# Routing queries in plain float32, and gate one-hots of four tokens in one comparison

## The chip, the cores and the metric

The kernel runs on one core of a Trainium2 chip. The metric is the device time in microseconds of one execution. Five engines work side by side, each through its own queue in order: TensorE (PE, with its weight loads as PEld), VectorE (DVE), ScalarE (ACT), GpSimd (POOL) and SyncE (SP), which issues most transfers.

## What is computed

One layer of a hybrid encoder over 1,024 tokens of width 1,024, then a final RMSNorm. A token mixer (stick-breaking attention and a gated delta net, merged by gates) and a cross-attention into 256 memory tokens come first. The third part, PEER retrieval, is the one that changes:

```
q = (xt @ w_pq).reshape(T, 8, 2, 128)              # routing queries
s = einsum('thpd,hpnd->thpn', q, subkeys)          # 128 scores per head and half
top_s, top_i = top_k(s, 16)
cand_s = top_s[:, :, 0, :, None] + top_s[:, :, 1, None, :]
best_s, best_pos = top_k(cand_s, 16)
expert = the pair of keys at best_pos;  gate = softmax(best_s)
act = gelu(einsum('thkd,td->thk', peer_u[expert], x)) * gate
out = einsum('thk,thkd->td', act, peer_v[expert])
```

## The kernel before

Tokens are worked in three groups, 256, 384 and 384 of them. Each group goes through token mixing, cross-attention and `routing`. A float32 product is made of three fast ones: `split` (lines 85 to 91) writes a value as a high and a low part, the high part by a copy on ScalarE (line 77), the low part by a subtraction on VectorE or GpSimd (line 89), and `mm3` (line 223) multiplies high by high, low by high and high by low. `proj` (from line 226) does this for each 128 columns of a weight matrix, which it loads as the tile `raw` and splits into `wh` and `wl`.

In `routing` the norm gives the activations `xn` and their parts `xhi` and `xlo` (in the last group `xh` and `xl`, which are kept). `proj` goes through the sixteen 128-column tiles of `w_pq`. For each tile ScalarE copies the queries out, TensorE multiplies them with the sub-keys (line 678), and `best` (lines 655 to 665) searches the sixteen best of 128 scores on VectorE, with five passes for each block of 128 tokens. The load of the next group's tokens (line 449, tile `gc`) waits for the last of these searches, because it takes over their memory.

Blocks 4, 5 and 6 of 128 tokens are retrieved by dense products over all 16,384 experts, the other five by gathers of expert rows (line 778), which GpSimd issues from the middle of the second group on, between everything else; VectorE reduces a gathered row in line 794 or adds it in line 83, TensorE weights it in line 823. For the dense blocks `spread` builds a matrix of gates: for each token a one-hot over the first key, times the gate (`o0`, line 898, VectorE), and a one-hot over the second key (`o1`, for even tokens on GpSimd in line 903, for odd ones in two steps on ScalarE), which TensorE multiplies (line 904). Four tokens share one PSUM bank, which ScalarE copies to `st`; with 384 tokens there are 96 such steps. Block 4's steps come from stored choices (`pick_stored`); those of blocks 5 and 6 follow their own choice (`pick_gates`) and are mixed with `dense_ahead`, which makes the first 36 of 128 dense tiles. `dense` then goes through all 128 tiles, mixed with the rest of the gathers.

The order of each engine's queue is written ahead of time by a planner that goes by its own costs for every instruction and keeps to the dependencies; nothing is reordered at run time.

Of the kernel before, what the change touches and what calls it, by code (L numbers as in the profile page):

```python
# [20 lines left out]
P = 128  # L21
# [15 lines left out]
OBS = 12  # L37
# [14 lines left out]
def block_kernel(ctx: ExitStack, tc: tile.TileContext, x_t, mem_t, gains, cst, sel, eye, w_in, conv, a_log,  # L52
# [22 lines left out]
    # ---- small helpers  # L75
# [42 lines left out]
    def mix(a, b, ratio):  # L118
        """Steps of a and b in turn, ratio of a for each of b."""
# [21 lines left out]
    # ---- constants  # L141
# [43 lines left out]
    # ---- scratch in DRAM  # L185
# [15 lines left out]
    # ---- building blocks  # L201
    def norm_t(hi, lo, tmp, xs, gi, n, keep=None):
        """RMSNorm over the partitions and tiles of xs(k), [P, n] each, split in two parts."""
# [7 lines left out]
        for k in range(KD):  # L211
            whole = keep is not None and keep.shape[2] == n
            y = keep[:, k] if whole else tmp.tile([P, n], F32, name="sq", bufs=2)
            stt(y, xs(k), gn[:, gi, k:k + 1], rs, OP.mult, OP.mult)
            split(hi[:, k], lo[:, k], y)
            if keep is not None and not whole:
                pool.tensor_copy(keep[:, k], y[:, n - keep.shape[2]:])
# [8 lines left out]
    def proj(w, col0, ncol, hi, lo, n, kt=KD, share=0):  # L226
        """Yields (tile index, product) for each 128 columns of w, transposed: [columns, tokens]. GpSimd splits
        every share-th tile of w."""
# [35 lines left out]
    # ---- stick-breaking attention of one 128-query block, four heads at a time, keys on partitions  # L264
    def stick(tmp, kT, vN, qT, sbo, e, qb, t0):
# [4 lines left out]
        for kb in range(qb, -1, -1):  # L270
# [6 lines left out]
            # softplus; for large z the logarithm is z itself  # L277
# [26 lines left out]
    # ---- gated delta net over one 128-token chunk, four heads together  # L304
    class Chunk:
# [67 lines left out]
        def inverse(self):  # L373
            """Inverse of (I + A) by doubling of diagonal blocks, and its transpose; AT holds -A transposed."""
# [26 lines left out]
            # keys and values with tokens on partitions  # L401
# [15 lines left out]
        def scan(self, S, S2, o):  # L417
            """Recurrence over chunks."""
# [17 lines left out]
    def token_mixing(g, t0, T, x1_where, result):  # L436
# [3 lines left out]
        with ExitStack() as eo:  # L440
# [11 lines left out]
            # gated delta net: projections, short convolution  # L452
# [9 lines left out]
            # beta and decay logits  # L462
# [65 lines left out]
            with ExitStack() as es:  # L528
                tmp = open_pool(f"d2{g}", 2, where=es)
                # output gate and branch gates wait in DRAM  # L530
# [104 lines left out]
    def routing(g, x1, t0, T, where, kept=None):  # L635
        """Returns the pool that choose() goes on with, and by block the best scores and keys."""
# [8 lines left out]
        if kept:  # L645
            hi, lo = kept
            n0 = sum(t0 // P + b in DENSE for b in range(NB)) * P
        else:
            n0 = 0
        with ExitStack() as es:  # L650
# [16 lines left out]
            xn = p1.tile([P, KD, T - n0], F32, name="xn")  # L667
            sk = p1.tile([P, 16, P], F32, name="sk")
            sp.dma_start(sk, subk)
            if not kept:  # L670
                hi, lo = p1.tile([P, KD, T], F32R, name="xhi"), p1.tile([P, KD, T], F32R, name="xlo")
            norm_t(hi, lo, tmp, lambda k: x1[:, k], 3, T, keep=xn)
            for i, ps in proj(w_pq, 0, 2048, hi, lo, T, share=SH_R):
# [8 lines left out]
            for src, dst in ((xn, xn_sc), (x1, xr_sc)):  # L682
                for b in range(NB):
# [4 lines left out]
                    c0 = b * P - (n0 if src is xn and kept else 0)  # L688
                    bs = slice(c0, c0 + P)
# [9 lines left out]
    def choose(tmp, tv, ti):  # L699
        """The sixteen best sums per head of one 128-token block. A pair (a, b) of ranks can be among them  # L700
        only with (a + 1) * (b + 1) <= 16: a < 4 with all b, or b < 4."""
# [21 lines left out]
        # gate: softmax over the chosen sixteen (the first is the largest)  # L723
# [7 lines left out]
        # position -> ranks -> expert  # L731
# [43 lines left out]
    # ---- retrieval by gathering expert rows  # L775
# [6 lines left out]
    def retrieve_u(blk, keep):  # L782
        """Expert activations of one block; tokens on partitions, one slot per gather."""
# [25 lines left out]
    def retrieve_v(blk, keep):  # L809
        """Weighted sum of expert rows, residual and final norm; slots on partitions, one token per gather."""  # L810
# [22 lines left out]
    def retrieve_y(blk, keep):  # L833
        """The same with tokens on partitions, one slot per gather."""
# [26 lines left out]
    def finish(y, ps, r0):  # L861
        """Final norm of 64 tokens, 32 w + p: quarter d of the channels of token (w, p) is y[32 d + p, w]."""
# [11 lines left out]
    # ---- retrieval by dense products over all experts, for the last tokens  # L874
    def choose_t(p2, tv, ti):
        """Keys and gates of one block with the slots on partitions."""
# [8 lines left out]
    def spread(px_, sel3, b):  # L885
        """Gates as a matrix: g_sc[c, i, r, t] is the gate of token 32 * c + t for expert 128 * r + i, zero if not
        chosen."""
        neg = px_.tile([P, 3, P], F32, name="neg")
        vec.tensor_scalar(neg[:, 0], sel3[:, 1], -1.0, None, op0=OP.mult)
        for c0 in range(0, P, 32):  # L890
            st = px_.tile([P, P, 32], F32, name="st")
            for c in range(c0, c0 + 32, 4):
                ps = by4(a_tile())
                for j in range(4):
                    o0 = px_.tile([P, P], F32, name="o0", bufs=OBS)
                    o1 = px_.tile([P, P], F32, name="o1", bufs=OBS)
                    t = c + j
# [225 lines left out]
```

## Time and profile before

| | us |
|---|---|
| median of three runs | 3813.43 (3813.3 to 3814.75) |
| span of the profiled execution, 56,994 instructions | 3821.6 |
| routing, first group (about) | 444 to 519 |
| routing, second group (about) | 1293 to 1413 |
| routing, third group (about) | 2324 to 2462 |
| spread (line 904), first to last | 2435 to 2808 |
| dense products (line 975), first to last | 2841 to 3779 |

The profiled execution was not timed beside its profile; its span stands 8.2 us over the median of the runs. Busy time is how long an engine had work running. Matmuls overlap each other, so the duration shown for one is longer than the distance from it to the next.

### The profile page before, as it was taken

Reading aid. Unit: us, or ns where it says so; the run is one execution under the profiler, and the core shown is the slowest. Engines: PE = TensorE matmul, PEld = TensorE weight load, DVE = VectorE, ACT = ScalarE, POOL = GpSimd, SP = SyncE. Lnnn points to the kernel's source line nnn. Section 1 sums busy time; section 2 is a strip of 40 time slices with the busy share of each in tenths; the row PEclk is TensorE's granted clock in tenths of the full one; section 3 lists DMA queues with packets and bytes.
Section 4 is the critical chain, followed back from the end, with each engine's and each line's share of the span. In section 5 each row is a group of like instructions: output and inputs, shape, how many; then the busy total and the mean of one; then the engine's idle time right before and its main releaser. Section 6 shows DMA issues by size and latency. Waiting matters only on the chain. (4 is left out here: it accounts for less than half of the span.)

```text
span 3821.6 us, 56994 instructions
## 1 busy us (share of the span) xinstructions
PE 3402.2 (89%) x20621; PEld 2852.3 (75%) x20621; DVE 2852.1 (75%) x5650; ACT 1624.2 (43%) x2992; POOL 1993.3 (52%) x1611
## 2 busy tenths in 40 slices
PE   7998977898889987999978899989769999999995
PEld 6888866787767765767766667878758888888884
DVE  6445699886566799427896667998767888887886
ACT  5754543664313333545523233556633333333333
POOL 1010007666754546467686455788964545544553
PEclk9999988998989988999979899999969999999997
DMA  6537539987899998989878989998999999999996
GB/s 163 147 92 210 151 110 316 332 293 235 290 353 300 347 335 282 307 301 305 263 248 288 345 301 341 305 315 275 325 316 330 340 339 347 339 327 321 360 386 236
DMA packets 745796, 1100.56 MB, mean 288 GB/s; under 512 B 42149, under 2 KB 554533, under 8 KB 742441
## 3 DMA queue, kind: packets, MB, share of 16 engines
q0 software_dynamic: 184320, 671.17, 49.4%
q1 hardware_dynamic: 561192, 425.73, 36.4%
q8 instruction: 163, 2.67, 0.3%
q14 instruction: 121, 0.98, 0.1%
HBM read 1036.60 MB, written 60.16 MB: 287 GB/s over the span
## 5 line engine op out<-in xcount | busy, mean ns | idle before, releaser
L778 POOL DMA_INDIRECT row<-in_peer_u_dram,ix x640 | 818.7, 1279 | 525.5 <-DVE y L83 146.9
L794 DVE CUSTOM_DVE_ANT_0 row<-row,xs 128x1024 f32<-128x1024 f32 x640 | 818.8, 1288 | 123.5 <-DMA row<-in_peer_u_dram,ix 100.9
L223 PE MATMUL pj<-xhi,wh 128*128 128x384 f32 (+1 forms) x1912 | 636.3, 333 | 52.9 <-ACT xhi L77 20.6
L223 PE MATMUL pj<-xhi,wl 128*128 128x384 f32 (+1 forms) x1912 | 637.0, 333 | 26.6 <-POOL wl L89 16.6
L89 DVE TENSOR_TENSOR wl<-raw,wh 128x1024 fp32r<-128x1024 f32 (+1 forms) x420 | 489.9, 1167 | 227.5 <-ACT wh L77 203.7
L778 POOL DMA_INDIRECT row<-in_peer_v_dram,it x384 | 448.6, 1168 | 358.3 <-PE ac L823 169.0
L223 PE MATMUL pj<-xlo,wh 128*128 128x384 f32 (+1 forms) x1912 | 621.4, 327 | 6.4 <-DVE xlo L89 6.4
L77 ACT ACTIVATE wh<-raw 128x1024 fp32r<-128x1024 f32 (+1 forms) x447 | 449.8, 1007 | 276.2 <-PE pj L223 176.5
L778 POOL DMA_INDIRECT row<-in_peer_v_dram,ix x256 | 352.0, 1375 | 346.7 <-DVE y L83 171.9
L223 PE MATMUL pj<-xh,wh 128*128 128x384 f32 x1152 | 399.9, 347 | 44.6 <-ACT h L80 41.6
L223 PEld LDWEIGHTS pj<-xhi,wh 128*128 128x128 f32 x1912 | 371.1, 194 | 89.6 <-ACT xhi L77 26.8
L223 PEld LDWEIGHTS pj<-xhi,wl 128*128 128x128 f32 x1912 | 370.9, 194 | 65.2 <-POOL wl L89 19.5
L223 PE MATMUL pj<-xh,wl 128*128 128x384 f32 x1152 | 398.8, 346 | 4.3 <-POOL wl L89 3.4
L223 PE MATMUL pj<-xl,wh 128*128 128x384 f32 x1152 | 393.1, 342 | 0.0
L223 PEld LDWEIGHTS pj<-xlo,wh 128*128 128x128 f32 x1912 | 369.4, 194 | 23.2 <-issue 10.6
L83 DVE SCALAR_TENSOR_TENSOR y<-row,hh,y 128x1024 f32<-128x1024 f32 x256 | 329.1, 1285 | 14.6 <-DMA row<-in_peer_v_dram,ix 13.1
L823 PE MATMUL ac<-row,sb 128*32 128x256 f32 x3072 | 267.0, 408 | 51.1 <-DMA row<-in_peer_v_dram,it 45.9
L89 POOL TENSOR_TENSOR wl<-raw,wh 128x1024 fp32r<-128x1024 f32 x27 | 66.0, 2443 | 428.1 <-DVE one L758 330.5
L77 ACT ACTIVATE vh<-vr 128x1024 fp32r<-128x1024 f32 x128 | 134.8, 1058 | 322.9 <-PE pj L975 311.6
L223 PEld LDWEIGHTS pj<-xh,wh 128*128 128x128 f32 x1152 | 220.3, 191 | 66.3 <-ACT h L80 56.9
L223 PEld LDWEIGHTS pj<-xh,wl 128*128 128x128 f32 x1152 | 220.7, 192 | 20.0 <-POOL wl L89 4.2
L89 DVE TENSOR_TENSOR vl<-vr,vh 128x1024 fp32r<-128x1024 f32 x128 | 156.5, 1223 | 90.7 <-ACT vh L77 79.3
(453 smaller groups left out, 6583.7 us busy)
## 6 DMA issues: line engine op xcount, KB each, us to landing
raw<-in_w_in_dram SPq DMA_DIRECT2D x132, 512.0 KB
raw<-in_peer_ut_dram SPq DMA_DIRECT2D x128, 512.0 KB
vr<-in_peer_v_dram SPq DMA_DIRECT2D x128, 512.0 KB
raw<-in_w_pq_dram SPq DMA_DIRECT2D x48, 512.0 KB
g_sc<-st SPq DMA_DIRECT2D x12, 2048.0 KB
gm<-g_sc SPq DMA_DIRECT2D x32, 768.0 KB
raw<-in_w_mix_dram SPq DMA_DIRECT2D x24, 512.0 KB
raw<-in_w_cq_dram SPq DMA_DIRECT2D x24, 512.0 KB
```

The source lines that it names most:

```text
L77: return act.activation(o, i, AF.Copy, scale=scale)
L83: return vec.scalar_tensor_tensor(out=o, in0=a, scalar=s, in1=b, op0=op0, op1=op1)
L89: eng.tensor_tensor(lo, src, hi, op=OP.subtract)
L223: pe.matmul(ps, lhsT=a[:, k], rhs=b[:, k], start=i == 0, stop=i == 3 * kt - 1)
L778: pool.indirect_dma_start(out=t, out_offset=None, in_=src, in_offset=bass.IndirectOffsetOnAxis(ap=index, axis=0))
L794: vec.tensor_tensor_reduce(out=t, in0=t, in1=xs, scale=1.0, scalar=0.0, op0=OP.mult, op1=OP.add, accum_out=hh[:, j:j + 1])
L823: pe.matmul(ac[32 * d:32 * d + 32, 256 * w:256 * w + 256], lhsT=sb[:, j], rhs=t[:, 256 * d:256 * d + 256], start=j == 0, stop=j == 31)
```

## The change

The routing queries are no longer made of three fast products of split operands: the raw weight tile and `xn`, both plain float32, are multiplied in one float32 product per 128 rows. The parts `xhi` and `xlo` go; in the last group the kept parts are made only for the 256 tokens of the dense blocks. `xn` covers all tokens of the group. In `spread` one VectorE comparison makes both one-hots of four tokens (1,024 numbers per partition), one GpSimd product weights the first half by the gates (512 numbers), and ScalarE has no part in it. The buffers hold three such steps, as they did before. Removed comments make up the rest of the diff.

```diff
-OBS = 12
+OBS = 3
@@ norm_t
-            whole = keep is not None and keep.shape[2] == n
-            y = keep[:, k] if whole else tmp.tile([P, n], F32, name="sq", bufs=2)
+            y = tmp.tile([P, n], F32, name="sq", bufs=2) if keep is None else keep[:, k]
             stt(y, xs(k), gn[:, gi, k:k + 1], rs, OP.mult, OP.mult)
-            split(hi[:, k], lo[:, k], y)
-            if keep is not None and not whole:
-                pool.tensor_copy(keep[:, k], y[:, n - keep.shape[2]:])
+            if hi is not None:
+                split(hi[:, k], lo[:, k], y)
@@ routing
-            xn = p1.tile([P, KD, T - n0], F32, name="xn")
+            xn = p1.tile([P, KD, T], F32, name="xn")
...
-            norm_t(hi, lo, tmp, lambda k: x1[:, k], 3, T, keep=xn)
-            for i, ps in proj(w_pq, 0, 2048, hi, lo, T, share=SH_R):
+            norm_t(None, None, tmp, lambda k: x1[:, k], 3, T, keep=xn)
+            if kept:
+                for k in range(KD):
+                    split(kept[0][:, k, :n0], kept[1][:, k, :n0], xn[:, k, :n0])
+            wv = w_pq.rearrange("(k p) c -> p k c", p=P)
+            for i in range(16):
+                raw = wp.tile([P, KD, P], F32, name="raw", bufs=3)
+                sp.dma_start(raw, wv[:, :, i * P:(i + 1) * P])
+                ps = j_tile()[:, :T]
+                for k in range(KD):
+                    pe.matmul(ps, lhsT=raw[:, k], rhs=xn[:, k], start=k == 0, stop=k == KD - 1)
@@ spread
-                for j in range(4):
-                    o0 = px_.tile([P, P], F32, name="o0", bufs=OBS)
-                    o1 = px_.tile([P, P], F32, name="o1", bufs=OBS)
-                    t = c + j
-                    vec.tensor_scalar(o0, io128, sel3[:, 0, t:t + 1], sel3[:, 2, t:t + 1], op0=OP.is_equal, op1=OP.mult)
-                    if j % 2:
-                        func(o1, io128, AF.Abs, bias=neg[:, 0, t:t + 1])
-                        func(o1, o1, AF.Relu, scale=-1.0, bias=1.0)
-                    else:
-                        pool.tensor_scalar(o1, io128, sel3[:, 1, t:t + 1], None, op0=OP.is_equal)
-                    pe.matmul(ps[:, j], lhsT=o1, rhs=o0, start=True, stop=True)
+                one = px_.tile([P, 2, 4, P], F32, name="one", bufs=OBS)
+                of = lambda t: t[:, :, c:c + 4, None].to_broadcast([P, t.shape[1], 4, P])
+                vec.tensor_tensor(one, io128[:, None, None, :].to_broadcast([P, 2, 4, P]), of(sel3[:, 0:2]), op=OP.is_equal)
+                pool.tensor_tensor(one[:, 0], one[:, 0], of(sel3[:, 2:3])[:, 0], op=OP.mult)
+                for j in range(4):
+                    pe.matmul(ps[:, j], lhsT=one[:, 1, j], rhs=one[:, 0, j], start=True, stop=True)
```

## Rows read from the trace of the kernel before

**Rows 1.** The page's first part: busy time, share of the span, instructions by engine

```profile
PE 3402.2 (89%) x20621; PEld 2852.3 (75%) x20621; DVE 2852.1 (75%) x5650; ACT 1624.2 (43%) x2992; POOL 1993.3 (52%) x1611
```

**Rows 2.** Busy time of each engine by stretch, from second routing to last spread

```profile
core 0: us, PE busy (x) PEld busy (x) DVE busy (x) ACT busy (x) POOL busy (x), PEclk, DMA share, GB/s
...
1350.00:1413.00 63.00, 52.29 (x375) 42.16 (x374) 63.00 (x286) 19.93 (x30) 30.48 (x28) 0.92 0.99 333
1413.00:1450.00 37.00, 22.02 (x92) 9.50 (x92) 37.00 (x178) 8.72 (x16) 22.26 (x18) 0.59 0.86 292
2336.00:2415.00 79.00, 76.97 (x534) 66.85 (x532) 75.12 (x296) 29.79 (x51) 43.00 (x39) 1.00 0.99 327
2415.00:2480.00 65.00, 59.86 (x406) 49.65 (x406) 63.47 (x257) 37.54 (x84) 50.48 (x48) 0.95 0.90 302
...
2480.00:2620.00 140.00, 124.37 (x810) 110.02 (x810) 132.45 (x417) 87.25 (x206) 112.03 (x107) 0.93 0.87 298
2620.00:2720.00 100.00, 97.79 (x663) 88.71 (x662) 80.97 (x178) 70.69 (x176) 88.67 (x89) 0.97 0.90 308
2720.00:2815.00 95.00, 52.02 (x269) 45.81 (x267) 70.72 (x134) 44.33 (x123) 85.89 (x79) 0.70 0.82 288
```

**Rows 3.** Timeline: the ends of the first two routings and the next load

```profile
453.44 2.76 DVE L89 TENSOR_TENSOR xlo<-xn,xhi 128x256 fp32r<-128x256 f32 x8
...
509.38 1.41 PE L678 MATMUL acc<-sk,sq 128*128 128x128 f32 x8
...
518.27 0.29 DVE L665 FIND_INDEX8 ti<-tv,s 128x8 uint32<-128x128 f32 x1
518.64 1.91 SPq L449 DMA_DIRECT2D gc<-in_x_t_dram  x4
...
1397.51 0.94 PE L678 MATMUL acc<-sk,sq 128*128 128x128 f32 x6
...
1413.05 0.28 DVE L665 FIND_INDEX8 ti<-tv,s 128x8 uint32<-128x128 f32 x1
...
2461.75 0.28 DVE L665 FIND_INDEX8 ti<-tv,s 128x8 uint32<-128x128 f32 x1
```

**Rows 4.** Timeline of TensorE: fast products at 256 and 384 columns, then plain float32

```profile
439.98 0.28 PE L223 MATMUL pj<-xhi,wh 128*128 128x256 f32 x1
...
440.33 0.28 PE L223 MATMUL pj<-xhi,wh 128*128 128x256 f32 x1
...
1304.23 0.34 PE L223 MATMUL pj<-xhi,wh 128*128 128x384 f32 x1
...
1304.75 0.34 PE L223 MATMUL pj<-xhi,wh 128*128 128x384 f32 x1
...
2263.20 2.85 PE L629 MATMUL pj<-pT,mV 128*128 128x384 f32 x8
2265.89 1.89 PE L614 MATMUL z<-mK,qT 128*128 128x256 f32 x8
2267.71 0.63 PE L823 MATMUL ac<-row,sb 128*32 128x256 f32 x6
```

**Rows 5.** VectorE: groups by form (subtractions), and all that touches the best scores

```profile
L89 DVE TENSOR_TENSOR wl<-raw,wh 128x1024 fp32r<-128x1024 f32 x372 | 457.0, 1229 | 212.3 <-ACT wh L77 190.9 <-issue 16.0 <-ACT h L80 1.9
...
0.00:3822.00 3822.00, 166.95 (x1040) 0.94 0.86 288
```

**Rows 6.** Groups by form: the one-hots on VectorE and GpSimd

```profile
L903 POOL TENSOR_SCALAR o<-io,sel 128x128 f32<-128x128 f32 x192 | 162.2, 855 | 9.9 <-PE acc L904 7.2 <-ACT sel L77 0.6
...
L898 DVE TENSOR_SCALAR o<-io,sel 128x128 f32<-128x128 f32 x384 | 139.5, 438 | 13.7 <-PE acc L904 12.6 <-PE ac L823 0.5
```

**Rows 7.** GpSimd with two inputs: min/median/max in ns, and beside VectorE

```profile
L370 POOL TENSOR_TENSOR D<-A,cs x32: 1252/1285/2304, 186.5 to 2031.4; 128x512 f32<-128x512 f32 x32
...
2665.17 3.01 DVE L898 TENSOR_SCALAR o<-io,sel 128x128 f32<-128x128 f32 x1
...
2665.70 2.40 POOL L89 TENSOR_TENSOR wl<-raw,wh 128x1024 fp32r<-128x1024 f32 x1
```

More of the change, by code (lines that the diff above doesn't have):

```diff
@@ L643, in found @@
             return tv[:, b], ti[:, b]
-        if kept:
-            hi, lo = kept
-            n0 = sum(t0 // P + b in DENSE for b in range(NB)) * P
-        else:
-            n0 = 0
+        n0 = sum(t0 // P + b in DENSE for b in range(NB)) * P if kept else 0
         with ExitStack() as es:
@@ L665, in best @@
                     vec.max_index(ti[:, b, i, 8:16], tv[:, b, i, 8:16], s1[:, b])
-            xn = p1.tile([P, KD, T - n0], F32, name="xn")
+            xn = p1.tile([P, KD, T], F32, name="xn")
             sk = p1.tile([P, 16, P], F32, name="sk")
             sp.dma_start(sk, subk)
-            if not kept:
-                hi, lo = p1.tile([P, KD, T], F32R, name="xhi"), p1.tile([P, KD, T], F32R, name="xlo")
-            norm_t(hi, lo, tmp, lambda k: x1[:, k], 3, T, keep=xn)
-            for i, ps in proj(w_pq, 0, 2048, hi, lo, T, share=SH_R):
+            norm_t(None, None, tmp, lambda k: x1[:, k], 3, T, keep=xn)
[9 more added lines that the diff above has]
+                    pe.matmul(ps, lhsT=raw[:, k], rhs=xn[:, k], start=k == 0, stop=k == KD - 1)
                 q = tmp.tile([P, T], F32, name="sq", bufs=2)
@@ L687, in routing @@
                         continue
-                    c0 = b * P - (n0 if src is xn and kept else 0)
-                    bs = slice(c0, c0 + P)
+                    bs = slice(b * P, (b + 1) * P)
                     e = tmp.tile([P, D], F32, name="tr", bufs=1)
@@ L885, in spread @@
     def spread(px_, sel3, b):
-        neg = px_.tile([P, 3, P], F32, name="neg")
-        vec.tensor_scalar(neg[:, 0], sel3[:, 1], -1.0, None, op0=OP.mult)
         for c0 in range(0, P, 32):
@@ L893, in spread @@
                 ps = by4(a_tile())
+                one = px_.tile([P, 2, 4, P], F32, name="one", bufs=OBS)
+                of = lambda t: t[:, :, c:c + 4, None].to_broadcast([P, t.shape[1], 4, P])
+                vec.tensor_tensor(one, io128[:, None, None, :].to_broadcast([P, 2, 4, P]), of(sel3[:, 0:2]), op=OP.is_equal)
+                pool.tensor_tensor(one[:, 0], one[:, 0], of(sel3[:, 2:3])[:, 0], op=OP.mult)
                 for j in range(4):
-                    o0 = px_.tile([P, P], F32, name="o0", bufs=OBS)
-                    o1 = px_.tile([P, P], F32, name="o1", bufs=OBS)
-                    t = c + j
-                    vec.tensor_scalar(o0, io128, sel3[:, 0, t:t + 1], sel3[:, 2, t:t + 1], op0=OP.is_equal, op1=OP.mult)
-                    if j % 2:
-                        func(o1, io128, AF.Abs, bias=neg[:, 0, t:t + 1])
-                        func(o1, o1, AF.Relu, scale=-1.0, bias=1.0)
-                    else:
-                        pool.tensor_scalar(o1, io128, sel3[:, 1, t:t + 1], None, op0=OP.is_equal)
-                    pe.matmul(ps[:, j], lhsT=o1, rhs=o0, start=True, stop=True)
+                    pe.matmul(ps[:, j], lhsT=one[:, 1, j], rhs=one[:, 0, j], start=True, stop=True)
                 copy(st[:, :, c - c0:c - c0 + 4], ps.rearrange("p j r -> p r j"))
```

## The prediction

> **What bounds the kernel now.** The page's first part [rows 1] comes first: TensorE is busy 89% of the span, VectorE 75%, GpSimd 52%. An average does not say what an edit is worth, so the second view is busy time by stretch [rows 2]. The bound changes hands. At the end of the second group's routing (1350 to 1413) VectorE is busy for all 63 us and TensorE for 52.29. From 1413 to 1450 VectorE still fills its 37 us, TensorE has 22.02, and its granted clock is 0.59, between its two levels. In the third group's routing (2336 to 2415) both are nearly full, TensorE 76.97 and VectorE 75.12 of 79. In the spread of the gates VectorE leads first (63.47 of 65 and 132.45 of 140), then TensorE (97.79 of 100), and at the end GpSimd (85.89 of 95), while TensorE has 52.02.
>
> The third view is the timeline at the end of a routing [rows 3]. In the first group TensorE's last product with the sub-keys ends at 510.8, VectorE's last search at 518.6, and the load of the next group's tokens is issued at 518.64, right behind it. In the second group the two ends stand at 1398.5 and 1413.3. So VectorE trails by 7.8 and 14.9 us, and it is the last search that lets the next group begin. In the third group the last search ends at 2462.0, and no next group waits for it, but the choices of blocks 5 and 6 do, and then their 64 steps of `spread`.
>
> **TensorE's price in routing.** At 384 columns three fast products take 0.52 us (1304.23 to 1304.75). Plain float32 shows two instructions for each product: the eight of line 629 take 2.69 us (2263.20 to 2265.89), 0.336 each, so one product costs 0.672. At 256 columns it is 0.35 against twice 0.2275 = 0.455 [rows 4]. These rows have other operands but the same shapes and types. The difference is 0.152 and 0.105 us for each of 8 x 16 products per group: +19.5 us in each of the two groups of 384, +13.4 us in the group of 256, 52.4 us in all. I take this as it stands; it is zero on the path only where another engine ends later anyway.
>
> **VectorE's relief in routing.** Sixteen subtractions of 1.229 us [rows 5] go in each group, 19.7 us, 59 in all, and as many ScalarE copies, which cost nothing, since ScalarE is far from full in every stretch [rows 2]. The activations' low parts go too: 2.76 us in the first group [rows 3], more by the columns in the second, a third of that in the last.
>
> **First group.** TensorE's end moves from 510.8 by +13.4, and back by 0 to 2.8, since the first products need not wait for low parts: 521.4 to 524.2. VectorE no longer trails by its whole backlog, only by the last tile: at most 166.95/128 = 1.3 us for each block's searches [rows 5], 2.6 for two. The last search ends at 524 to 527 instead of 518.6. Some of this the planner can hide by another order, so I take +5.5, bounds 0 and +8. Next late is the load of line 449 and everything behind it.
>
> **Second group.** In the same way: 1398.5 + 19.5, less 0 to 4 us for the activations' parts (2.76 x 384/256), plus 3.9 for three blocks, is 1418 to 1422 instead of 1413.3. I take +7, bounds 0 and +9. VectorE's 19.7 us are worth nothing beyond its 14.9 us of lag, since TensorE is then the later of the two.
>
> **Third group and spread.** Here TensorE has other work to move: `dense_ahead` fills gaps, and from 2720 on TensorE is idle for 43 of 95 us [rows 2]. So its +19.5 us are covered, at a price of up to 19.5 if the planner does not move these tiles. What sets the end is VectorE to 2620, then GpSimd. VectorE loses the 19.7 us of subtractions. A step of `spread` costs it 139.5/96 = 1.45 us now [rows 6]; the one comparison over 1,024 numbers is as large as a subtraction, 1.23 us [rows 5]. That saves 0.22 us a step, some 45 steps of the 96 (its share of the time) lying before 2620: 10 us.
>
> Against it stands a new collision. The GpSimd product with two inputs over 512 numbers costs 1.25 us or more [rows 7]. In the one place where I looked closely, GpSimd's subtraction runs from 2665.70 for 2.40 us, and a VectorE comparison that started at 2665.17 lasts 3.01 us, to the end of it [rows 7]; its group's mean is 0.438 [rows 6]. So VectorE stands still while GpSimd works on two tensors. The price per step is between 0 (VectorE happens to wait for something else) and 1.25 us (always next in line). GpSimd has such products now in a few places only; after the change there are 96 of them, right where VectorE is fullest. I take 0.7, nearer to the row than to nothing. A step then costs VectorE 1.23 + 0.7 = 1.93, +0.48, and 45 steps +21.6.
>
> The Trainium skill (SBUF — State Buffer, section "SBUF: two separate sides") says that VectorE and GpSimd share one pair of ports, which is locked for a whole instruction whenever VectorE has two inputs in SBUF or runs in a two-port mode and GpSimd reads there. By that rule the comparison and the product can never overlap. The trace agrees in the row of 3.01 us; how often the two meet, no row shows.
>
> GpSimd's own queue: two comparisons a step cost 162.2/96 = 1.69 us now [rows 6], one product 1.25 (the least) to 1.29 (the median) [rows 7]. The product also has to wait for VectorE's comparison, which the old ones did not; the gathers queued behind it on GpSimd wait with it, and VectorE waits for those rows in turn. From 2720 on, where GpSimd is the bound, some 23 steps save 0 to 10 us; I take 4. ScalarE's two passes per odd token go for nothing gained directly.
>
> Sum for this part: -19.7 + 21.6 - 4 is about -2; I call it 0, bounds -34 (all relief, no collision: -19.7 - 10 - 4) and +46 (45 x (1.25 - 0.22) alone, relief swallowed by a TensorE-bound routing).
>
> **Sum.** +5.5 + 7 + 0 = +12.5 us on the profiled span of 3821.6. That span stands 8.2 us over the median; I carry the difference over to the median: 3813.4 + 12.5, about 3826 us. The dense stage behind it gets no different work.
>
> **The rivals.** A difference of 0.2%, 7.6 us, is about what a measurement of this kernel can tell from none.
>
> 1. Faster: VectorE's relief wins in the third group. The place is 2336 to 2620, where VectorE is busy for 271.04 of 284 us [rows 2]. If a GpSimd product costs VectorE less than 0.22 us, a step gets cheaper, the 19.7 us stay saved, and -34 comes near; with some 25 us of it, 12.5 - 25 gives 3801 us. For it speaks how full VectorE is there; against it the row of 3.01 us. The sign turns where the third part saves more than the 12.5 us that the first two groups lose.
>
> 2. Slower by more: the lock. If VectorE is next in line nearly always, a step costs it 1.23 + 1.25 = 2.48 instead of 1.45, 45 steps +46 us; less 19.7 - 4 = 23.7 that is +22, with the first two groups +35: 3848 us. This is what the rule of the skill's page gives when both engines always have work. For it speaks that both are at 80% and more from 2480 to 2620; against it, that VectorE's searches and waits leave room.
>
> 3. No change that can be measured: the planner hides the first two groups' delays, because the searches, the choices and the next norm can be put in another order, and the third part comes out even: 0 to +5, 3813 to 3819 us. For it speaks that gathers fill much of each queue and can be moved; against it, that the load of the next group hangs on the last search [rows 3].
>
> That the float32 product is not made as rows 4 show it would take away the 52.4 us altogether and belongs to the first rival.
>
> **Chances.** The forecast 0.38, the first rival 0.28, the second 0.21, the third 0.13. The forecast's own range is 3817 to 3836, and a fifth of it lies within 0.2%. So faster 0.28, same 0.20, slower 0.52. The range has to reach over the first and most of the second rival: 3792 to 3862 us.
>
> **What would show it.** In the routing products, two instructions of about 0.336 us each per product at 384 columns, and no subtraction of `w_pq` tiles. The last search about 3 to 5 us behind TensorE's last product in the first two groups, the next load right behind it, and 5 to 8 us later than now. In `spread`, VectorE's comparisons with a mean well over 1.23 us, and gather reductions of 1.2 us that last 2 or more beside a GpSimd product; if both stay near 1.23, the first rival is right. The prediction is wrong if the second group starts no later, or if TensorE has to wait for raw weight tiles, of which only three are now in flight and each is held until TensorE is done with it.

## The result, and the profile after

The changed kernel took 3924.12 us (median of four runs, 3910.93 to 3930.45) against 3814.09 for the kernel before, run beside it: the ratio is 1.0283, 95% interval 1.0255 to 1.0310. It is 108 us slower, far outside the predicted range. One of the twelve executions of e14 below took 14,314 us, nearly four times the others, and is left out of its ratio. The execution profiled here took 3922.76 us, with a span of 3921.0.

The page's first part of the changed kernel (columns as in [rows 1]):

```profile
PE 3445.8 (88%) x20237; PEld 2828.8 (72%) x20237; DVE 2847.8 (73%) x5295; ACT 1466.9 (37%) x2539; POOL 1957.6 (50%) x1507
```

Hardly any busy time has been added. TensorE has 44 us more; VectorE has 4, GpSimd 36 and ScalarE 157 us less, and still the span has grown by 99 us. So the loss is in what stands idle, or in instructions that last longer than their work needs, and where.

The first place to look is the end of the routings, against [rows 3]. The timeline of the changed kernel, first group (two lines) and second group (four):

```profile
520.19 0.71 PE L679 MATMUL acc<-sk,sq 128*128 128x128 f32 x4 [0.94 <-ACT sq L77]
...
526.95 1.39 SPq L447 DMA_DIRECT2D gc<-in_x_t_dram  x3
...
1406.57 2.36 PE L823 MATMUL ac<-row,sb 128*32 128x256 f32 x38
1408.86 0.94 PE L679 MATMUL acc<-sk,sq 128*128 128x128 f32 x6
...
1421.23 0.29 DVE L659 FIND_INDEX8 ti<-tv,s 128x8 uint32<-128x128 f32 x1
1421.59 1.40 SPq L447 DMA_DIRECT2D gc<-in_x_t_dram  x3
```

The loads of the next group stand at 526.95 and 1421.59 instead of 518.64 and 1413.4: later by 8.3 and 8.2 us. Both are delays against the kernel before and don't add up. The first routing began 3.1 us late and added 5.2, close to the forecast. The second began 6.8 us late (its sub-keys are loaded at 1294.9 instead of 1288.1) and added 1.4, where 7 was forecast. The line to keep in mind is the 38 matmuls of line 823, the products of gathered rows: TensorE does them in a heap when the queries are done.

The price of the float32 product is seen in TensorE's timeline, to hold against [rows 4]:

```profile
479.76 3.40 PE L674 MATMUL pj<-xn,raw 128*128 128x256 f32 x15
483.00 0.61 PE L679 MATMUL acc<-sk,sq 128*128 128x128 f32 x4
...
1344.36 5.97 PE L674 MATMUL pj<-xn,raw 128*128 128x384 f32 x18
1350.16 0.71 PE L694 MATMUL z<-cs,x 128*128 128x128 f32 x5
```

From start to next start, 18 instructions take 5.80 us, 0.322 each and 0.644 for a product of 384 columns; at 256 columns it is 3.24/15 x 2 = 0.432. Against 0.52 and 0.35 that is 128 x 0.124 = 15.9 us for a group of 384 and 10.5 for the first, 42 us in all.

Busy time by stretch (columns as in [rows 2]), for the second and third routing and the spread. First the kernel before, in two stretches that were not shown yet:

```profile
1300.00:1413.00 113.00, 102.29 (x724) 86.35 (x722) 110.88 (x465) 40.04 (x65) 56.70 (x49) 0.94 0.99 337
...
2340.00:2475.00 135.00, 127.83 (x875) 109.31 (x873) 129.69 (x516) 61.95 (x121) 86.28 (x79) 0.97 0.94 313
```

and the changed kernel:

```profile
1300.00:1413.00 113.00, 108.90 (x503) 66.89 (x502) 76.07 (x397) 26.46 (x50) 25.34 (x25) 1.00 0.71 227
...
2340.00:2475.00 135.00, 133.69 (x621) 90.18 (x622) 94.03 (x442) 39.09 (x77) 31.20 (x29) 1.00 0.67 217
2475.00:2620.00 145.00, 120.62 (x809) 102.62 (x808) 144.81 (x326) 53.71 (x74) 108.19 (x74) 0.94 0.77 265
2620.00:2720.00 100.00, 90.79 (x572) 80.00 (x571) 87.92 (x92) 34.54 (x51) 77.80 (x52) 0.93 0.89 301
...
2890.00:3775.00 885.00, 843.10 (x4148) 747.70 (x4148) 718.73 (x859) 302.90 (x412) 421.96 (x319) 0.99 1.00 345
```

In both routings TensorE is now full (133.69 of 135), VectorE has lost some three tenths of its work, and the DMA share falls from 0.99 and 0.94 to 0.71 and 0.67. From 2890 on it is 1.00: what the transfers have not made by then finds no free place there. From 2475 to 2720 there still was some, at 0.77 and 0.89.

What is missing is in GpSimd's gathers. The same view for line 778 alone (busy time and count on GpSimd, then clock, DMA share and GB/s of the stretch), the second routing, the third and the time from 3775 on; before, then after:

```profile
1300.00:1413.00 113.00, 56.70 (x49) 0.94 0.99 337
2340.00:2475.00 135.00, 64.88 (x53) 0.97 0.94 313
3775.00:3940.00 165.00, 5.61 (x5) 0.87 0.13 47
```

```profile
1300.00:1413.00 113.00, 25.34 (x25) 1.00 0.71 227
2340.00:2475.00 135.00, 28.80 (x26) 1.00 0.67 217
3775.00:3940.00 165.00, 64.33 (x49) 0.81 0.72 256
```

24 and 27 gathers are gone from the two routings, and 44 more stand after 3775. A gather moves 671.17 MB / 1280 = 0.524 MB (the page's third part), so at 341 GB/s it takes 1.54 us of all the transfers: 51 of them are 79 us.

The last stretch begins at a fixed time, and the changed kernel is late by then. Here are the gathers of line 778 cut at each run's own stages, with e1, which has the new routing and the old spread (see below). The tail runs from the last dense product to the end.

| gathers | up to the third routing's last search | up to the first dense product | dense stage | tail | tail, us |
|---|---|---|---|---|---|
| before | 827 | 117 | 331 | 5 | 42.5 |
| e1 | 784 | 126 | 333 | 37 | 88.2 |
| changed kernel | 784 | 143 | 333 | 20 | 65.9 |

When the routings are over, both are 43 gathers behind. The dense stage, at a DMA share of 0.99 to 1.00, takes about the same number in all three, and the rest stands behind it: 32 and 15 more than before, 49 and 23 us at 1.54 each. The tails are 46 and 23 us longer.

Who holds them up is told by GpSimd's waits in the third routing (us in total, times, longest), before and after:

```profile
POOL row L778 <- PE ac L823: 25.8, 13, 3.5
```

```profile
POOL row L778 <- PE ac L823: 57.7, 4, 28.7
```

A gather needs a free row buffer, and TensorE frees it with the product of line 823. Before, these came between the query products at short intervals; after, GpSimd once waits 28.7 us for one.

The spread took 426 us from its first matmul to its last, 373 before. Groups by form of that stretch in the changed kernel:

```profile
L894 DVE TENSOR_TENSOR one<-io,sel 128x1024 f32<-128x1024 f32 x93 | 141.9, 1534 | 32.5 <-PE acc L897 25.7 <-POOL one L895 6.8
...
L895 POOL TENSOR_TENSOR one<-one,sel 128x512 f32<-128x512 f32 x93 | 117.6, 1272 | 22.9 <-DVE one L894 21.9
...
L794 DVE CUSTOM_DVE_ANT_0 row<-row,xs 128x1024 f32<-128x1024 f32 x65 | 94.5, 1460 | 13.8 <-DMA row<-in_peer_u_dram,ix 13.8
```

and a piece of its timeline, first VectorE, then GpSimd:

```profile
2689.88 4.99 DVE L894 TENSOR_TENSOR one<-io,sel 128x1024 f32<-128x1024 f32 x1 [0.33 <-PE acc L897]
2694.79 1.21 DVE L794 CUSTOM_DVE_ANT_0 row<-row,xs 128x1024 f32<-128x1024 f32 x1
2695.93 0.08 DVE L794 DVE_READ_ACCUMULATOR2_ANT hh<- 128x1 f32 x1
2695.93 2.05 DVE L894 TENSOR_TENSOR one<-io,sel 128x1024 f32<-128x1024 f32 x1
```

```profile
2690.42 2.37 POOL L89 TENSOR_TENSOR wl<-raw,wh 128x1024 fp32r<-128x1024 f32 x1
2692.73 1.04 POOL L895 TENSOR_TENSOR one<-one,sel 128x512 f32<-128x512 f32 x1
2693.93 1.78 POOL L778 DMA_INDIRECT row<-in_peer_u_dram,ix  x1 [0.16 <-issue]
2695.72 1.18 POOL L895 TENSOR_TENSOR one<-one,sel 128x512 f32<-128x512 f32 x1
```

A comparison takes 1.20 us at least and 1.22 in the median. The one at 2689.88 lasts 4.99 us and ends 1.1 us after GpSimd is through a subtraction and a product; the next one, beside the product at 2695.72, 2.05. The gather at 2693.93 takes 1.78 us.

Taken over the whole program, the delay against the kernel before is 24.8 us at the start of the third routing, 13.1 at its last search, 80.5 at the last matmul of the spread, 78.8 at the first dense product, 76.0 at the last product of the dense stage and 99.4 at the end. Two thirds arise in the spread, and another 23 us in the tail, where the displaced gathers stand.

### The profile page after: what moved, and what is told of

Its sections match the earlier page's. It is cut to its first block, busy times and chain, and to the rows that moved or that the text cites. A ratio compares the mean times of both kernels' runs of the same rounds, so it can differ in the third digit from the quotient of the medians.

```text
span 3921.0 us, 55216 instructions
## 1 busy us (share of the span) xinstructions
PE 3445.8 (88%) x20237; PEld 2828.8 (72%) x20237; DVE 2847.8 (73%) x5295; ACT 1466.9 (37%) x2539; POOL 1957.6 (50%) x1507
## 3 DMA queue, kind: packets, MB, share of 16 engines
q0 software_dynamic: 184320, 671.17, 48.3%
## 5 line engine op out<-in xcount | busy, mean ns | idle before, releaser
L221 PE MATMUL pj<-xhi,wh 128*128 128x384 f32 (+1 forms) x1656 | 561.2, 339 | 56.1 <-ACT xhi L77 21.9
L89 DVE TENSOR_TENSOR wl<-raw,wh 128x1024 fp32r<-128x1024 f32 (+1 forms) x372 | 438.5, 1179 | 234.5 <-ACT wh L77 234.2
L221 PE MATMUL pj<-xhi,wl 128*128 128x384 f32 (+1 forms) x1656 | 560.8, 339 | 33.3 <-POOL wl L89 24.5
L221 PE MATMUL pj<-xlo,wh 128*128 128x384 f32 (+1 forms) x1656 | 547.0, 333 | 5.1 <-DVE xlo L89 5.1
L77 ACT ACTIVATE wh<-raw 128x1024 fp32r<-128x1024 f32 (+1 forms) x399 | 399.5, 1002 | 274.9 <-PE pj L221 192.3
L221 PEld LDWEIGHTS pj<-xhi,wh 128*128 128x128 f32 x1656 | 325.9, 197 | 94.6 <-ACT xhi L77 28.5
L221 PEld LDWEIGHTS pj<-xhi,wl 128*128 128x128 f32 x1656 | 326.3, 197 | 66.4 <-POOL wl L89 27.3
L221 PE MATMUL pj<-xh,wl 128*128 128x384 f32 x1024 | 353.6, 345 | 19.8 <-DVE wl L89 14.9
L221 PEld LDWEIGHTS pj<-xlo,wh 128*128 128x128 f32 x1656 | 324.5, 197 | 26.7 <-issue 12.0
L674 PE MATMUL pj<-xn,raw 128*128 128x384 f32 (+1 forms) x768 | 230.4, 451 | 4.7 <-DVE xn L83 4.7
```

Of the source, the lines that this page charges most:

```text
L77: return act.activation(o, i, AF.Copy, scale=scale)
L221: pe.matmul(ps, lhsT=a[:, k], rhs=b[:, k], start=i == 0, stop=i == 3 * kt - 1)
L674: pe.matmul(ps, lhsT=raw[:, k], rhs=xn[:, k], start=k == 0, stop=k == KD - 1)
```

## The experiments

All ratios are to runs of the kernel before on the same chip; the differences in us are the ratio less 1, times 3814. Lines of code are shortened.

| run | plain float32 in groups | gate product | ratio (95% interval) | us |
|---|---|---|---|---|
| changed kernel | 1, 2, 3 | GpSimd | 1.0283 (1.0255 to 1.0310) | +108 |
| e1 routing only | 1, 2, 3 | old spread | 1.0203 (1.0175 to 1.0232) | +77 |
| e2 spread only | none | GpSimd | 1.0188 (1.0156 to 1.0221) | +72 |
| e3 | 1, 2, 3 | VectorE | 1.0198 (1.0169 to 1.0226) | +76 |
| e4 | 1, 2, 3 | ScalarE | 1.0169 (1.0142 to 1.0196) | +64 |
| e5 | none | ScalarE | 0.9979 (0.9968 to 0.9990) | -8 |
| e6 | 1, 2 | old spread | 1.0132 (1.0103 to 1.0162) | +50 |
| e7 | 1, 2, half of 3 | old spread | 1.0124 (1.0098 to 1.0150) | +47 |
| e8 | 1, 2, 3, row products first | old spread | 1.0127 (1.0104 to 1.0150) | +48 |
| e9 | none | GpSimd, by a constant | 1.0228 (1.0199 to 1.0258) | +87 |
| e10 | none | GpSimd, four buffers | 1.0134 (1.0111 to 1.0157) | +51 |
| e11 | 1 | old spread | 1.0036 (1.0020 to 1.0053) | +14 |
| e12 | 1, 2, 3, some row products first | old spread | 1.0139 (1.0112 to 1.0167) | +53 |
| e13 | none | GpSimd, half | 1.0061 (1.0037 to 1.0085) | +23 |
| e14 | none | ScalarE, four buffers | 0.9959 (0.9947 to 0.9972) | -16 |
| e15 | 1, half of 2 and 3 | old spread | 1.0041 (1.0020 to 1.0062) | +16 |

### Which half of the change

e1 keeps the routing of the change and puts the old `spread` back; e2 does the opposite.

> The routing of the changed kernel (plain float32 products, no splits) with the spread of the kernel before. The changed kernel takes 110 us more than the one before (3924 against 3814). Theory A, the loss is made in the spread, by 96 GpSimd products with two inputs beside a full VectorE: then routing alone costs what the first two groups show, about +5 and +1 us at the ends of their routings, and wins part of the 19.7 us that VectorE is relieved of in the third: 3795 to 3830. Theory B, the loss comes from routing (TensorE's 52 us more, and what is displaced by it): 3870 to 3925.

> The routing of the kernel before with the spread of the changed kernel (one comparison for four tokens, the gate product on GpSimd). Theory A, the loss is made in the spread: from the last search to the last matmul of the spread it is 67 us longer in the changed kernel, and the tail after the dense stage 23 us, so 3880 to 3930. Theory B, the loss comes from routing: 3800 to 3830.

Theory A gave e1 at most 3830 us, and that fell: each half by itself costs over 70 us. Together they cost 108 and not 149, so they overlap. The gathers cut by stages show part of it: e1 and the changed kernel leave the routings equally far behind, and the longer spread of the changed kernel lets 17 gathers more through than e1's, 26 us at 1.54 of the 41 that are shared. The rest was not isolated. In e1 the first dense product is only 13 us later than before, and 46 us more stand behind the dense stage. Line 778 in e1:

```profile
1300.00:1413.00 113.00, 24.37 (x25) 0.98 0.71 227
...
2340.00:2475.00 135.00, 26.70 (x25) 1.00 0.63 208
...
3775.00:3940.00 165.00, 49.76 (x45) 0.74 0.48 174
```

The gathers are missing in the same two places with the old spread. It is the routing that drives them out.

### Routing: one group at a time, and half the products

e6 and e11 use the old routing for some groups. e7 and e15 leave the weights' loads as they are and take TensorE's work out, by summing over half of the rows. Other experts are chosen by that, but as many are gathered.

```diff
+    pool_c, found = (routing_old if last else routing)(g, ...)           # e6
+    pool_c, found = (routing if g == 0 else routing_old)(g, ...)         # e11
-    for k in range(KD):
+    for k in (range(0, KD, 2) if kept else range(KD)):                   # e7; e15: if g > 0
         pe.matmul(ps, lhsT=raw[:, k], rhs=xn[:, k], ...)
```

> Plain float32 routing in groups 1 and 2 only; the third group's routing and the spread are those of the kernel before. With float32 routing in all groups and the old spread it took 74 us more; the trace then has 25 gathers from 2340 to 2475 us instead of 53, a DMA share of 0.63 instead of 0.94, and 45 gathers instead of 5 behind the dense stage. Theory A, gathers pushed out of the third routing are paid back at the end, where DMA is full: the gathers stay in their place here, and only the +5 and +1 us of the first two routings remain, 3815 to 3830. Theory B, the delay of the first two groups shifts the whole plan: 3860 or more.

> Float32 routing with the old spread, where the third group's queries are summed over every second of the eight 128-row parts alone: 64 float32 products, 43 us of TensorE, are left out, the weights are loaded as before. Theory A, a TensorE without a gap leaves no place for the products of the gathered rows (line 823), and so the row buffers aren't freed and GpSimd's gathers stand: with half the work most of the 53 gathers come back into the third routing, 15 or fewer are left behind the dense stage, 3800 to 3835. Theory B, it is the weight tiles, held until TensorE is done with them, or the order of the plan as such: some 25 gathers and 3865 or more, less what TensorE saves itself.

> Plain float32 routing in group 1 alone; everything else is the kernel before. In groups 1 and 2 together it took 49 us more, and the second routing let 27 gathers pass instead of 49, while no gather is under way yet in the first. Theory A, displaced gathers are the loss (some 1.5 us each at the end, where the DMA engines are full: 22 x 1.5 = 33): group 1 alone costs about its own +5 us, 3815 to 3832. Theory B, any delay of an early group is multiplied by the plan behind it: 3840 to 3870.

> Float32 routing in all groups with the old spread; in groups 2 and 3 the queries are summed over every second of the eight 128-row parts, so that 43 us of TensorE are left out in each; the weights are loaded as before. With the half sum in group 3 alone it took 48 us more than the kernel before, against 74 with full sums, and its second routing still let 24 gathers pass instead of 49. Theory A, a TensorE that is full in a routing pushes gathers out of it, some 1.5 us each at the end: then the gathers are back in both routings and what remains is group 1's +11 us less what the shorter routings save: 3800 to 3835. Theory B, something else in the new routing (weight tiles held longer, the order of the plan): 3850 or more.

The counts of gathers, from the view shown above:

| | second routing | third routing | from 3775 us on | us |
|---|---|---|---|---|
| before | 49 | 53 | 5 | |
| e1 | 25 | 25 | 45 | +77 |
| e6 | 27 | 54 | 22 | +50 |
| e7 | 24 | 57 | 21 | +47 |
| e11 | 50 | 56 | 5 | +14 |
| e15 | 48 | 51 | 10 | +16 |

e6 missed its 3815 to 3830, because I had not seen that the second routing drives gathers out too; e7 missed its 3800 to 3835 for the same reason, and e11 and e15 ended 7 and 2 us above theirs. With that the sums fit roughly; each difference is uncertain by 13 to 16 us. From e11 to e6 the second group is added: 23 gathers go, 23 x 1.54 = 35 us, and the time rises by 36. From e6 to e1 the third is added: 29 gathers, 45 us by the same price, and 27 measured. The price shows directly only in the tails above. In e6 the tail holds 6 gathers against 5 before, and 33 us of the delay are there at the first dense product; by what way the second group's gathers come into these was not found.

e15 brings the gathers back in both routings, with the weight tiles loaded as in e1, and +61 of the 77 us go. Half a sum takes 64 x 0.644 = 41 us of TensorE out of a routing, more than the 15.9 that the change put in, so the 61 us are not the price of these alone. But the gathers go by TensorE's fullness, not by the weight tiles: of the waits that TensorE has in e1's second and third routing, none is for a weight tile.

e11's +14 us is more than the 5.5 predicted for the first group. In its trace the next load comes 9 us later than before, and the old spread took 387 us instead of 373; in eight plans with that spread it took 362 to 391, so plans differ by some 10 us for reasons that I did not follow.

### Routing: the order of TensorE's queue

```diff
+    with tc.high_priority():        # e8: all tokens; e12: some
         for d in range(4):
             pe.matmul(ac[32 * d:32 * d + 32, ...], lhsT=sb[:, j], ...)
```

> Float32 routing with the old spread; the only difference is that the plan puts the TensorE products of gathered rows (line 823) ahead of other work that is ready. No work is added or left out. Theory A: gathers stood because these products came last in TensorE's queue, though they are short (8 us for 82 of them); put first, they cost the third routing 5 to 10 us and bring back the 25 missing gathers, so the tail falls from 90 us to 45 to 55: 3825 to 3850. Theory B, TensorE's own 52 us are the loss: 3880 to 3900 as without it.

> Float32 routing in all groups, old spread; the plan puts TensorE's products of gathered rows first only for the tokens that fall into the second and third routing (from token 92 on in block 0, tokens 60 to 103 in block 2). With all of them first the gathers came back (53 and 67 in the two routings) and the tail went, but group 2's mixing, in which such products now also came first, took 24 us more, and the time was 3871. Theory A, the order alone is the loss, apart from TensorE's price on the path: group 2 starts its routing at most 5 us later than in the kernel before, the gathers are back, and the time is 3830 to 3855. Theory B, TensorE has no room in its routing for them, and what they gain is lost there: 3865 to 3885.

Line 778 in e12:

```profile
1300.00:1413.00 113.00, 58.95 (x55) 1.00 0.98 341
...
2340.00:2475.00 135.00, 75.13 (x68) 1.00 0.99 346
...
3775.00:3940.00 165.00, 3.75 (x4) 0.89 0.25 86
```

e8, with all of these products first, brought the gathers back (53 and 67) and still took +48 us, above its 3825 to 3850. In e12, too, the gathers are all back, the DMA share is 0.98 and 0.99, the tail is as short as before, and the time is still +53 us: theory B. The second routing, from the load of the sub-keys to the next group's load, takes 158 us instead of 126 in e1. Some of it is the products themselves, and some is waiting: TensorE takes its queue in order and stood there 10.8 us for gathered rows that had not arrived. So the order alone was not the loss, as I had put it in e12. TensorE, full in these stretches (111.12 of 113 us in e12's second), has no room for both, and the plan only chooses who pays.

### Spread: who makes the product

```diff
-    pool.tensor_tensor(one[:, 0], one[:, 0], gates, op=OP.mult)
+    vec.tensor_tensor(one[:, 0], one[:, 0], gates, op=OP.mult)              # e3
+    for j in range(4):                                                      # e4, e5, e14
+        copy(one[:, 0, j], one[:, 0, j], sel3[:, 2, c + j:c + j + 1])
-OBS = 3
+OBS = 4                                                                     # e10, e14
```

> The changed kernel with the gate product on VectorE in place of GpSimd: 96 products of 512 numbers with two inputs leave GpSimd and are added to VectorE. Theory A1, the two engines shut each other out: VectorE gets 96 products more (by half of its comparison of 1.21 us for 1,024 numbers an estimate of 0.6 us each, 60 us) but its comparisons and gather reductions go back to 1.22 to 1.29 us and GpSimd's gathers to 1.0 us: 3840 to 3880, and the collision is worth the difference to 3924. Theory A2, what costs is that each step goes from VectorE over GpSimd to TensorE and stands there behind gathers: then also faster, but with comparisons of 1.5 us as they are now. Theory B, the routing: 3924 or more, because VectorE gets work on top.

> The changed kernel with the gate product on ScalarE, four copies of 128 numbers with the gate of one token as scale in place of one GpSimd product. ScalarE is busy 33% of the time from 2475 to 2890 in the changed kernel. Theory A1, GpSimd and VectorE shut each other out: the comparisons go back to 1.22 us, GpSimd's gathers to 1.0 us, the spread takes no longer than before, and the time is 3790 to 3830. Theory A2, the chain of three engines in each step with only three buffers is what costs: it stays, with ScalarE in place of GpSimd, and most of the 67 us with it: 3880 to 3925. Theory B, the routing: 3900 to 3925.

> The kernel before, with only the one-hots made anew: one VectorE comparison for four tokens, and the gates multiplied in by ScalarE (four copies). With the new routing this spread took 365 us from its first matmul to its last, against 373 in the kernel before and 426 with the GpSimd product; what was left of the loss there (+26 us at the first dense product, +22 in the tail) I put down to the third routing. Theory A, then nothing is left of the loss: 3795 to 3818. Theory B, the VectorE comparison alone holds up GpSimd (its gathers take 1.42 us in that stretch, not 1.0) and that is paid for: 3825 to 3850.

> The spread of the changed kernel with the old routing, with four buffers of one-hots in place of three. Theory A1, the engines shut each other out: 3870 to 3890, as with three. Theory A2, the chain's length over three buffers sets the step (VectorE stands 22 us for TensorE to free a buffer, TensorE 121 us for GpSimd's product in the changed kernel): a quarter of the 446 us of the spread is to be had at most, and 20 us or more of it show: 3860 or less.

e3 and e4 still have the new routing and stay near e1: on top of it the GpSimd product costs 31 us (108 against 77), a VectorE product nothing, a ScalarE product -13 (the intervals overlap). So both missed the times of theory A1, which left the routing's loss out; what it said of the comparisons came: their mean from 2475 to 2840 is 1.31 us in e3 and 1.29 in e4. e5 shows the same without the new routing: e2 and e5 differ only in who multiplies, and the time goes from +72 to -8. A fourth buffer (e10) takes 21 of e2's 72 us. The two intervals overlap slightly, and the 3876 us themselves lie in the range of theory A1; if the gain holds, part of the loss is that three steps of buffers do not cover the chain.

### Spread: length or place of the product

```diff
-    pool.tensor_tensor(one[:, 0], one[:, 0], gates, op=OP.mult)
+    pool.tensor_scalar(one[:, 0], one[:, 0], 1.0, None, op0=OP.mult)                    # e9
+    pool.tensor_tensor(one[:, 0, 0:2], one[:, 0, 0:2], gates_of_two, op=OP.mult)        # e13
```

> The spread of the changed kernel with the old routing (which took 70 us more than the kernel before), but GpSimd's step multiplies its 512 numbers by the constant 1: one input tensor in place of two, the same place in the chain, the same buffers. The gates are left out of the matrix. Theory A1, GpSimd's use of two tensors shuts VectorE out: VectorE's comparisons fall from 1.62 us to about 1.3, its gather reductions from 1.55 to 1.22, and the time to 3810 to 3835. Theory A2, it is the place in GpSimd's queue and the chain VectorE, GpSimd, TensorE that costs: 3870 to 3890 as with two inputs.

> The spread of the changed kernel with the old routing, but GpSimd's product covers two of the four tokens (256 numbers instead of 512); the gates of the other two tokens of each step are left out. Its place in the chain and the buffers stay. From the first to the last matmul of the spread VectorE was busy for 412 of 447 us with the full product and for 326 of 375 in the kernel before. Theory A1, VectorE stands still for as long as GpSimd's product runs: half a product gives back about half of the 70 us, 3840 to 3860, and the comparisons' mean falls from 1.62 us to about 1.4. Theory A2, the place in GpSimd's queue costs, whatever the product's length: 3870 to 3890.

Groups by form over the spread in e2, e13 and e9, in this order:

```profile
L894 DVE TENSOR_TENSOR one<-io,sel 128x1024 f32<-128x1024 f32 x93 | 146.3, 1581 | 25.5 <-PE acc L897 21.9 <-POOL one L895 2.5 <-PE pj L223 1.1
...
L895 POOL TENSOR_TENSOR one<-one,sel 128x512 f32<-128x512 f32 x93 | 127.6, 1378 | 27.2 <-DVE one L894 25.7 <-issue 0.5
```

```profile
L894 DVE TENSOR_TENSOR one<-io,sel 128x1024 f32<-128x1024 f32 x93 | 127.3, 1380 | 18.1 <-PE acc L897 18.0
...
L895 POOL TENSOR_TENSOR one<-one,sel 128x256 f32<-128x256 f32 x93 | 97.4, 1057 | 24.0 <-DVE one L894 21.1 <-issue 1.9
```

```profile
L895 POOL TENSOR_SCALAR one<-one 128x512 f32<-128x512 f32 x93 | 170.5, 1838 | 9.6 <-DVE one L894 8.1
...
L894 DVE TENSOR_TENSOR one<-io,sel 128x1024 f32<-128x1024 f32 x93 | 123.5, 1332 | 31.9 <-PE acc L897 27.6 <-POOL one L895 3.0 <-issue 1.1
```

The product of half the length, at the same place in both queues, gives back 49 of 72 us. So it is the length and not the place. VectorE's comparison follows it: 1.58 us with the full product, 1.38 with half, 1.31 in e5 with none on GpSimd.

How much of the 72 us is VectorE's is seen in its busy time from the first to the last matmul of the spread, in e2, e13 and e5 (columns as in [rows 2]):

```profile
2424.00:2871.00 447.00, 327.40 (x1992) 288.00 (x1991) 412.40 (x634) 136.97 (x205) 356.87 (x237) 0.83 0.81 275
...
2431.00:2834.00 403.00, 313.88 (x1993) 279.35 (x1991) 370.30 (x636) 136.66 (x204) 316.78 (x238) 0.86 0.90 308
...
2437.00:2812.00 375.00, 312.61 (x1995) 276.37 (x1993) 337.01 (x634) 246.00 (x577) 223.42 (x146) 0.91 0.94 332
```

VectorE has 634 instructions there in e2 as in e5, and in e2 they last 75 us longer; the kernel takes 80 us more. In e13 it has 636, they last 33 us longer than in e5, and the kernel takes 31 us more. So the lengthening of VectorE's instructions matches nearly all of the difference. Only a third of it lies in the comparisons (146.3 us against 120.9); as much lies in 69 gather reductions (107.6 against 83.5), none of which lasts over 1.26 us in e5.

VectorE's standing still is not the only way to lose time there. In e9, which leaves the gates out, the comparison is nearly as free (1.33 us), but GpSimd takes 1.84 us for the simpler operation and is busy for 414 of the spread's 466 us. TensorE waits 112 us for it, and the time is the longest of these runs instead of the 3810 to 3835 of theory A1. VectorE has 400 us there, so both engines are near full; which of them sets the pace in e9 was not separated.

### The version that beats both

> The kernel before with one comparison for four tokens and the gates multiplied in by ScalarE, with four buffers in place of three. With three it took 0.21% less than the kernel before. VectorE waited 23 us in that spread for TensorE to free a buffer. If these waits lie on the path, 5 to 15 us come back: 3800 to 3810. If the spread there is held by the transfers (DMA share 0.94) it stays at 3812 to 3818.

e14 takes 0.41% less than the kernel before (0.28 to 0.53%), 16 us; its spread takes 357 us instead of 373. Its 3808 us lie in the expected range. The one-hots in one comparison for four tokens are worth having, with the product on ScalarE, a fourth buffer and the old routing; what each of these parts gives was not measured. Whether the buffer alone made the step from e5 to e14 isn't settled: the intervals overlap.

## Why the prediction was wrong

**The collision in the spread: the mechanism right, the size wrong.** The forecast's third term was 0, with bounds of -34 and +46. It charged the collision to 45 steps, +21.6 us after the gain of the cheaper comparison. The spread alone cost +72 (e2), and 80 against the same spread with the product on ScalarE (e5). The step that failed is the count, with what it left out. The 45 steps are those before the point where GpSimd took over as the bound in the old profile [rows 2]; in e2 VectorE is busy for 412 of the spread's 447 us, so all 96 count. The price of 0.7 us was near by luck: 75 us over 96 products are 0.78, but the comparison, which was to bear it, lost 0.36 in the mean (1.58 against a median of 1.22). The rest fell on VectorE's other work, which the sum left out (gather reductions of 1.57 us in e2, 1.21 in e5). The second rival had the mechanism at full price, but with the same 45 steps it came to 3848 us.

**The rule of the lock.** The rows show a comparison that takes 1.20 us at least and here lasts 4.99 beside GpSimd's subtraction and product. The rule in the Trainium skill (SBUF — State Buffer, section "SBUF: two separate sides"), that such operations shut each other out for a whole instruction, agrees with these rows. By it I should have counted every product, wherever VectorE has work. In e9, where GpSimd's operation reads one tensor, the comparison's mean (1.33 us) is hardly above e5's without it (1.31): there VectorE does not stand still.

**Third group: TensorE's +19.5 us "are covered".** This is the step that failed outright. I looked for work that TensorE could move and found `dense_ahead`. I did not ask what TensorE's short products of gathered rows do for others: they free the row buffers, and GpSimd's gathers, which the DMA engines need to stay full, stand without them. Group 3 in float32 cost 27 us (e1 less e6, uncertain by 16).

**Second group: +7.** As a later end it did not come: the routing itself took 1.4 us longer. TensorE made room for its longer products by letting products of gathered rows go: 104 of its matmuls of line 823 stand between 1300 and 1413 instead of 208. With them 23 gathers were driven out (e6) of a stretch that had used the DMA engines at 0.99, and the group cost 36 us (e6 less e11). The transfers' share stood in the stretches that I read [rows 2] and had no place in the sum.

**First group: +5.5.** The routing itself took 5.2 us longer (8.3 less 3.1 that it began late). By itself the edit measures +14 (8 to 20 by its interval); no gather is under way there.

**TensorE's price: 52.4.** It is 42 us by the pitch shown above; the mechanism (two instructions for a product) holds.

**VectorE's relief.** It came: 76.07 us busy instead of 110.88 in the second routing, 94.03 instead of 129.69 in the third. Little came of it, since TensorE was then full. The third routing's last search was 11.7 us less late than its start; how much of that is this relief and how much the row products that left the routing, no run separates. The first rival lived on this relief and fell.

**The dense stage "gets no different work".** Its length is the same (938 us before, 935 after), but 15 gathers more stand behind it, and the tail is 23 us longer by that.

**The signs.** The two instructions for a product came, and VectorE's lengthened comparisons and reductions did. The last search stood 6.0 and 11.7 us behind TensorE's last product with the sub-keys, where 3 to 5 was forecast. In the routings TensorE waited for no weight tile.

## What to carry to other kernels

Before costing an edit on an engine that is nearly full, list what its small instructions release for others: here TensorE products that took 18 us of the old third routing kept the transfers going, and transfers that a stage does not make come back at the end if a later stage has a DMA share of 1.00 (32 gathers and 46 us in e1's tail). A stretch in which three resources are each above 0.9 has no cover to give, whatever the average says. And a two-input operation on GpSimd beside a full VectorE is to be counted for every instance and against all of VectorE's work, here about 0.8 us for each of 96; ScalarE had the room.

## What the runs showed of the hardware

- GpSimd's product of 512 numbers with a constant, one input tensor, took 1.48 us at least and 1.65 in the median; the product of two tensors of that size took 1.03 and 1.17 in the changed kernel. Fewer inputs did not make it shorter.
- 96 two-input products of 512 numbers on GpSimd went with 412 us for VectorE's 634 instructions of the spread (e2); with the product on ScalarE as many took 337 (e5).
- A gather's issue on GpSimd lasts longer in the spreads with VectorE's two-input comparisons, even where GpSimd makes no product: from 2475 to 2840 us the first kind of gather (from `peer_u`) takes 1.26 us in the mean in the kernel before, 1.50 in e2, 1.43 in e5 and 1.36 in e4. The medians are 1.03, 1.72, 1.49 and 1.16.
- A row product put early in TensorE's queue can cost more than its own time: in e12 TensorE stood 10.8 us, in three waits between 1300 and 1455, for rows that were still under way.
